# Residual tiles of two projections: loaded plainly ahead of their sums, every product added by VectorE, two kinds of stores issued from other engines

## The chip, the core and the metric

The kernel runs on one core of a Trainium2 chip. The metric is device time in microseconds (us) of one execution, from a median of several runs. The engines are TensorE (PE, with PEld for its weight loads), VectorE (DVE), ScalarE (ACT), GpSimd (POOL) and SyncE (SP). DMAs can be issued from SP, ACT and POOL; each of these issues in the order of its own instruction queue, and an instruction that waits holds up all that stand behind it on the same engine.

## The reference

One layer of a hybrid encoder on 512 tokens of width 2048, all in float32. An mLSTM branch and a differential-attention branch are computed from a common input projection, gated, and mixed; what matters here comes after:

```
x  = x + (g_m * branch_m + g_a * branch_a) @ w_out     # 2048 x 2048, "wo"
h2 = rmsnorm(x, norm2_w)
gate, up = split(h2 @ w_ffn_in)                         # 2048 x 11264, "fi"
x  = x + (silu(gate) * up) @ w_ffn_out                  # 5632 x 2048, "fo"
return rmsnorm(x, final_norm_w)
```

The two lines that begin with `x = x +` are residual sums. Their first operands (the input `x` in the first, the `x` after the first sum in the second) are called residual tiles here: [128 tokens x 512 columns], 16 of them in each sum.

## The kernel before, in words

**Arithmetic.** Every float32 operand is split into a high and a low part of type fp32r: ScalarE casts the high part (line 149), VectorE subtracts it from the source to get the low part (line 150). A product is three matmuls (high x high, high x low, low x high, line 145). Large products are made by `seven`, a seven-product (Strassen-Winograd) scheme over 2x2 blocks: per group of 512 rows of the weight there are the products Q1, Q5, Q6, then Q2, Q3, Q7, and at the end Q4, each 12 matmuls of 128x128x512. Sums of raw weight blocks (lines 348, 356, 362, 369) and of operand blocks are VectorE's.

**Order.** `seven` runs over all groups with Q1, Q5, Q6, then over all groups with Q2, Q3, Q7 (in the last group Q7, Q3, Q2), then over all groups with Q4. Each product accumulates over the groups in one of three pairs of PSUM banks (`BANK`: a for Q1 and Q2, b for Q6, Q7, Q4, c for Q5 and Q3). After the last group of a product, `post` takes the bank's sum away. "wo" has 4 groups, and two chunks (wo0, wo1) of 1024 output columns each. "fo" has 10 groups in the seven-product scheme and an eleventh in plain products (W12, W22, W11, W21, with a further pair of banks d), again in two chunks (fo0, fo1). "fi" lies between wo1 and fo0: 11 chunks.

**Weights.** Raw weight blocks (512 KB each) come by SP's DMAs (line 197) into a ring of buffers, 6 to 8 loads ahead of use; a buffer is free when VectorE has read it last. `take` makes pieces two ahead of use (`AHEAD = 2`).

**Time in the program.** The program's own clock is advanced by each step (`tick`; a product step counts 12 x 216 ns). `later(ns, fn)` puts a step off by so much of that clock, and `when` / `behind` / `work` hand out one small step per product. The instructions on each engine are then put in order by a list scheduler, so neighbours can change places.

**Buffers.** `t_` tiles (128x512, float32) come from one pool of 39; a tile that finds no free one waits for the last reader of an older tile.

**The step that changes.** `added` (line 791) makes `post` for wo and fo. Output blocks are named 11, 12, 21, 22. After Q1, ScalarE copies bank a three times for each of two token tiles (six copies, line 813) into the tiles 22, 12 and 21, with sign; Q5, Q6, Q7, D, Q3, Q4 are added or subtracted by VectorE (lines 816 to 837). The residual tile enters 21 right after Q1, 12 after Q3, and 22 after Q7 (wo) or D (fo), by a DMA from POOL that adds the DRAM tile to the tile in SBUF (`accum_op`, line 802). Block 11 is different: its residual tile is loaded plainly after Q5 (line 817), and Q2 is added to it by VectorE. `final` of the blocks 22 and 12 is put off by `later(8000, ...)`, that of 11 and 21 follows at once.

In wo, `final` stores the sum to DRAM from POOL (`x1d`, line 883), squares it on ScalarE (line 885) and, when two token tiles are there, has `turned` 2 us of program time later: TensorE transposes them (line 849), ScalarE scales them out of PSUM (line 858) and stores them from its own queue (line 860); for the columns of wo0 VectorE makes four sums of the turned blocks (line 863), which SP stores (line 864). wo1 loads these again at its Q2 (line 494, from POOL). In fo, `final` squares on ScalarE (line 1004), multiplies by the final norm's weight, and with the fourth tile of a token row scales and stores the output. During fo POOL also loads fi's results (line 988), each of which is split by ScalarE and VectorE.

Of the kernel before, what the change touches and what calls it, by code (L numbers as in the profile page):

```python
# [14 lines left out]
AF = mybir.ActivationFunctionType  # L15
ALU = mybir.AluOpType
# [11 lines left out]
NFB = DFF // 512  # L28
# [86 lines left out]
def build(ctx, tc, a, out):  # L115
    nc = tc.nc
    V, A, G, T = nc.vector, nc.scalar, nc.gpsimd, nc.tensor
# [97 lines left out]
    def later(ns, fn):  # L215

        tasks.append((clock[0] + ns, fn))
        tasks.sort(key=lambda t: t[0])
# [337 lines left out]
    xs, q, vals, sig, mqk, mval, has, hms = [], {}, {}, {}, {}, {}, [], []  # L556
# [232 lines left out]
    x1d = [[dpool.tile([P, 512], F32, name=f"x1d{t}_{c}") for c in range(4)] for t in range(NT)]  # L789

    def added(nm, n, src, final, plain=False):
        x = {}

        def tile_(q, i):
            x[q, i] = t_(f"{nm}_x{q}{i}")
            return x[q, i]

        def place(q, i):
            return (i if q < 20 else 2 + i), 2 * n + (q - 1) % 10

        def fetch(q, i):
            G.dma_start(x[q, i], src(*place(q, i)), accum_op=ALU.add)

        def end(q, i):
            t, c = place(q, i)
            final(t, c, x[q, i])

        def post(q_, bank):
            a_, b_, c_ = (bank[k] for k in "abc")
            for i in range(2):  # L810
                if q_ == "Q1":
                    for q, sc in ((22, -1.0), (12, -1.0), (21, 1.0)):
                        A.activation(tile_(q, i), a_[i], AF.Copy, scale=sc)
                    fetch(21, i)
                elif q_ == "Q5":
                    V.tensor_tensor(x[22, i], x[22, i], c_[i], ALU.add)  # L816
                    G.dma_start(tile_(11, i), src(*place(11, i)))
                elif q_ == "Q6":
                    V.tensor_tensor(x[12, i], x[12, i], b_[i], ALU.subtract)
                elif q_ == "Q7":  # L820
                    V.tensor_tensor(x[22, i], x[22, i], b_[i], ALU.subtract)
                    if not plain:
                        fetch(22, i)
                        later(8000, lambda i=i: end(22, i))
                elif q_ == "D":
                    V.tensor_tensor(x[22, i], x[22, i], bank["d"][i], ALU.add)
                    fetch(22, i)
                    later(8000, lambda i=i: end(22, i))
                elif q_ == "Q3":
                    V.tensor_tensor(x[12, i], x[12, i], c_[i], ALU.add)  # L830
                    fetch(12, i)
                    later(8000, lambda i=i: end(12, i))
                elif q_ == "Q2":
                    V.tensor_tensor(x[11, i], x[11, i], a_[i], ALU.add)
                    end(11, i)
                else:
                    V.tensor_tensor(x[21, i], x[21, i], b_[i], ALU.add)  # L837
                    end(21, i)
        return post

    def turned(nm, src, cols, out, i, keep, scale=None):

        for j in (1, 2):
            f_ = f"X{i + 1}{j}"
            tp = ps(f"{nm}_T{i}{j}")
            for k in range(2):
                kk = 2 * k + j - 1
                for t in range(2):
                    T.transpose(tp[:, k * 256 + t * P:k * 256 + (t + 1) * P],
                                src[t][:, cols + kk * P:cols + (kk + 1) * P], ident)  # L850
            out[f_] = half(f"{nm}_{f_}")
            tv = tp.rearrange("p (k c) -> p k c", k=2)
            if scale is None:
                A.copy(out[f_], tv)
            else:
                for k in range(2):
                    kk = 2 * k + j - 1
                    A.activation(out[f_][:, k], tv[:, k], AF.Copy, scale=scale(kk))
            if keep and f_ in keep:
                nc.scalar.dma_start(keep[f_].rearrange("p (k c) -> p k c", k=2), out[f_])  # L860
        if keep and "S1" in keep and len(out) == 4:
            def sum_(f_, to, l, r, op):
# [17 lines left out]

    def wo_chunk(n):
        def final(t, c, x):
            G.dma_start(x1d[t][c], x)
            j = t_(f"x1j{t}_{c}")
            A.activation(j, x, AF.Square, accum_out=ss2p[:, t * 4 + c:t * 4 + c + 1])
            x1[t, c] = x
            i = t // 2
            if (2 * i, c) in x1 and (2 * i + 1, c) in x1:
                pair = [x1.pop((2 * i + k, c)) for k in range(2)]
                later(2000, lambda: turned(f"h2{c}", pair, 0, h2X[c], i,  # L890
                                           h2d[c] if n == 0 else None,
                                           lambda kk: n2w[:, c * 4 + kk:c * 4 + kk + 1]))

        def start(q_):
            if n == 1 and q_ == "Q2":
                for g in range(4):
                    h2f[g] = {}
                p0, p1 = (loaded(f"h2{c}", c, h2f[c], h2d[c]) for c in range(2))
                p2, p3 = (kept(f"h2{c}", c, h2f[c], h2X[c]) for c in (2, 3))
                ahead([p0[0], p1[0], p0[1]])  # L900
                for c, p in ((3, p3), (2, p2)):
                    when(lambda c=c: len(h2X[c]) >= 4, p[0])
                when(lambda: True, [p1[1][0]] + p1[1][1])
                when(lambda: True, p3[1] + p2[1])

        seven(f"wo{n}", lambda g, h_, l: a["w_out"][n, g, h_, l], range(4), lambda g: mixf[g],
              added(f"wo{n}", n, lambda t, c: a["x"][t][:, c * 512:(c + 1) * 512], final), start)

    def rstd2():
        ss2 = sm("ss4", NT, bufs=2)  # L910
# [90 lines left out]
    def fo_chunk(n):  # L1001
        def final(t, c, x):
            j = t_(f"x2j{t}_{c}")
            A.activation(j, x, AF.Square, accum_out=ss3p[:, t * 4 + c:t * 4 + c + 1])  # L1004
            mine = fin.setdefault(t, [])
            mine.append((c, x))
            if len(mine) < 4:
                later(0 if n else 30000, lambda: V.tensor_tensor(x, x, env["fnw"][c], ALU.mult))  # L1008
                tick(0)
                return  # L1010
            ss = sm("ss1", 1)
            V.tensor_reduce(ss, ss3p[:, t * 4:t * 4 + 4], AX.X, ALU.add)
# [12 lines left out]
        def start(q_):  # L1025
            if q_ == "Q4" and n == 0:
                env["fnw"] = [t_(f"fnw{c}") for c in range(4)]
                for c in range(4):
                    G.dma_start(env["fnw"][c],
                                a["fnw"][:, c * 512:(c + 1) * 512].broadcast_to([P, 512]))  # L1030
        seven(f"fo{n}", lambda g, h_, l: a["w_ffo"][n, g, h_, l], GR, lambda g: fgf[n, g],
              added(f"fo{n}", n, lambda t, c: x1d[t][c], final, True), start, NFB - 1, True)

    fin = {}

# [281 lines left out]
    for k in range(KD):  # L1317
# [159 lines left out]
```

## Time and profile before

| | |
|---|---|
| time, median of 3 runs | 2661.37 us (2660.05 to 2668.32) |
| the profiled execution, its own time | 2664.15 us |
| its span | 2662.4 us |
| mean granted TensorE clock | 0.994 |
| busy: PE / DVE / ACT / POOL | 2599.0 / 2106.5 / 1308.8 / 253.7 us |
| wo0 and wo1, fi, fo0 and fo1 (from the span's start) | 1158 to 1337, 1337 to 2204, 2204 to 2652 us |

All rows come from the one profiled execution. Times in the timeline are from the span's start. A row of the timeline is: start, duration, engine, line, operation, tile written <- tiles read, shape, and in brackets the engine's idle time before it with what ended that. "x6" says that six neighbours are merged. In a row of the waits stand: who waited <- for whom: us in total, times, longest us. In a row of a window PEclk is the granted share of the TensorE clock, DMA share the mean busy share of the 16 DMA engines.

### The profile page before, as it was taken

How to read it: one execution, taken by the hardware profiler on the slowest of the kernel's cores; microseconds unless marked ns; L12 is line 12 of the kernel's file. 1: busy time of each engine (PE TensorE's matmuls, PEld its weight loads, DVE VectorE, ACT ScalarE, POOL GpSimd, SP SyncE). 2: the span in 40 equal slices, each digit the busy share in tenths (PEclk: the TensorE clock that was granted, in tenths of full speed). 3: DMA queues.
4: the chain of work that ended last, by engine and by line, in shares of the span. 5: the costliest groups of instructions: out<-in, count | busy, mean ns of one | idle time of the engine just before them, and what ended most of it. 6: DMA issues, size and time to landing. Idle time of an engine off the chain costs nothing. (4 is left out here: it accounts for less than half of the span.)

```text
span 2662.4 us, 33245 instructions
## 1 busy us (share of the span) xinstructions
PE 2599.0 (98%) x12184; PEld 2160.8 (81%) x12184; DVE 2106.5 (79%) x2660; ACT 1308.8 (49%) x1848; POOL 253.7 (10%) x448
## 2 busy tenths in 40 slices
PE   7999999999999999998999999999999999999997
PEld 6878888878889988887778888888888878787886
DVE  8977888788875675686788888788888879879885
ACT  8544444545543543354564444444444436646554
POOL 1000000011210122101200000000000001222211
PEclk9999999999999999999999999999999999999999
DMA  7655566744432345447755554565555577777763
GB/s 250 237 187 181 201 200 208 240 119 126 132 104 88 125 158 208 169 150 233 216 203 180 188 195 165 177 211 181 186 190 186 176 281 276 251 256 257 239 224 91
DMA packets 162227, 508.97 MB, mean 191 GB/s; under 512 B 21832, under 2 KB 22120, under 8 KB 162064
## 3 DMA queue, kind: packets, MB, share of 16 engines
q1 hardware_dynamic: 111456, 379.77, 41.6%
q0 software_dynamic: 33712, 97.71, 12.3%
q10 hardware_dynamic: 16896, 29.37, 3.2%
q8 instruction: 95, 1.56, 0.2%
q14 instruction: 68, 0.56, 0.1%
HBM read 445.41 MB, written 50.87 MB: 186 GB/s over the span
## 5 line engine op out<-in xcount | busy, mean ns | idle before, releaser
L145 PE MATMUL aqk_b<-xs,whi_aqk 128*128 128x512 f32 x512 | 161.6, 396 | 0.0
L149 ACT CAST whi_fi_Q<-fi_Q_t 128x1024 fp32r<-128x1024 f32 x88 | 92.5, 1052 | 116.7 <-PE fi_b L145 98.3
L145 PE MATMUL fi_a<-whi_fi_Q,h_X 128*128 128x512 f32 x440 | 147.2, 392 | 0.0
L145 PE MATMUL fi_c<-whi_fi_Q,h_S 128*128 128x512 f32 x440 | 144.6, 390 | 0.0
L145 PE MATMUL fi_b<-whi_fi_Q,h_S 128*128 128x512 f32 x352 | 115.6, 389 | 0.0
L145 PEld LDWEIGHTS aqk_b<-xs,whi_aqk 128*128 128x128 f32 x512 | 94.6, 189 | 18.3
L150 DVE TENSOR_TENSOR wlo_fi_Q<-fi_Q_t,whi_fi_Q 128x1024 fp32r<-128x1024 f32 x88 | 106.2, 1217 | 4.1 <-ACT whi_fi_Q L149 4.1
L362 DVE TENSOR_TENSOR raw_fi_e<-raw_fi_e,raw_fi_f 128x1024 f32<-128x1024 f32 x44 | 53.9, 1224 | 65.0 <-DMA raw_fi_e<-in_w_ffi 64.9
L145 PE MATMUL aqk_b<-xs,wlo_aqk 128*128 128x512 f32 x256 | 100.5, 393 | 0.0
L145 PEld LDWEIGHTS fi_c<-whi_fi_Q,h_S 128*128 128x128 f32 x440 | 82.6, 188 | 17.1
L145 PEld LDWEIGHTS fi_a<-whi_fi_Q,h_X 128*128 128x128 f32 x440 | 82.6, 188 | 16.8
L988 POOL DMA_DIRECT2D fs_X<-fg_X11d x22 | 11.8, 538 | 830.2 <-DVE wlo_fi_Q L150 785.5
L145 PE MATMUL fi_a<-wlo_fi_Q,h_X 128*128 128x512 f32 x220 | 86.0, 391 | 1.9 <-DVE wlo_fi_Q L150 1.8
L348 DVE TENSOR_TENSOR raw_fi_b<-raw_fi_b,raw_fi_a 128x1024 f32<-128x1024 f32 x44 | 53.8, 1223 | 41.5 <-DMA raw_fi_b<-in_w_ffi 36.7
L145 PE MATMUL fi_c<-wlo_fi_Q,h_S 128*128 128x512 f32 x220 | 86.0, 391 | 0.6 <-DVE wlo_fi_Q L150 0.5
L145 PE MATMUL ba_p<-whi_ba,hahl 128*128 128x512 f32 x256 | 82.5, 392 | 0.0
L149 ACT CAST whi_fi_Q<-raw_fi_e 128x1024 fp32r<-128x1024 f32 x44 | 46.4, 1055 | 73.1 <-PE fi_b L145 48.2
L149 ACT CAST whi_fi_Q<-raw_fi_b 128x1024 fp32r<-128x1024 f32 x44 | 46.5, 1056 | 69.5 <-PE fi_c L145 51.9
L145 PE MATMUL bm_p<-whi_bm,hmhl 128*128 128x512 f32 x256 | 80.5, 392 | 0.0
L145 PE MATMUL mqk_b<-xs,whi_mqk 128*128 128x512 f32 x256 | 80.4, 394 | 0.0
L149 ACT CAST whi_fi_Q<-raw_fi_f 128x1024 fp32r<-128x1024 f32 x44 | 46.4, 1055 | 67.4 <-PE fi_c L145 65.3
L145 PEld LDWEIGHTS fi_b<-whi_fi_Q,h_S 128*128 128x128 f32 x352 | 66.1, 188 | 13.6
(837 smaller groups left out, 8452.3 us busy)
## 6 DMA issues: line engine op xcount, KB each, us to landing
raw_fi_a<-in_w_ffi SPq DMA_DIRECT2D x44, 512.0 KB, 3.7
raw_fi_b<-in_w_ffi SPq DMA_DIRECT2D x44, 512.0 KB, 4.2
raw_fi_c<-in_w_ffi SPq DMA_DIRECT2D x44, 512.0 KB, 4.4
raw_fi_d<-in_w_ffi SPq DMA_DIRECT2D x44, 512.0 KB, 4.2
raw_fi_f<-in_w_ffi SPq DMA_DIRECT2D x44, 512.0 KB, 3.8
raw_fi_e<-in_w_ffi SPq DMA_DIRECT2D x44, 512.0 KB, 4.2
raw_aqk<-in_w_aqk SPq DMA_DIRECT2D x32, 512.0 KB, 3.6
raw_fo_a<-in_w_ffo SPq DMA_DIRECT2D x20, 512.0 KB, 4.8
```

The source lines that it names most:

```text
L145: T.matmul(dst, lhs[l], rhs[r], start=first and i == 0, stop=last and i == 2, skip_group_check=skip)
L149: A.copy(hi, src)
L150: V.tensor_tensor(lo, src, hi.bitcast(F32), ALU.subtract)
L348: V.tensor_tensor(raws[r12], raws[r12], raws[r11], ALU.add)
L362: V.tensor_tensor(raws[r12], raws[r12], raws[r22], ALU.add)
L988: G.dma_start(got[n], fgd[g][f_].rearrange("p (k c) -> p k c", k=2))
```

## The change

All six tiles that Q1 goes into are loaded with their residual tiles beforehand, by plain DMAs from POOL, 10 us (wo) or 66 us (fo) of program time after the first Q1 of the chunk; the two tiles of block 11 likewise 12 us or 70 us after the first Q2. VectorE adds or subtracts every product, Q1 too, straight onto them: six VectorE operations in place of six ScalarE copies in each of the four chunks. There is no accumulating DMA and no `later(8000, ...)`: `final` follows the last product of each block at once. `x1d` is stored from ScalarE's queue, behind the square; the four sums of the turned blocks of wo0 are stored from POOL in place of SP.

```diff
     def added(nm, n, src, final, plain=False):
         x = {}
-        def tile_(q, i):
-            x[q, i] = t_(f"{nm}_x{q}{i}")
-            return x[q, i]
...
-        def fetch(q, i):
-            G.dma_start(x[q, i], src(*place(q, i)), accum_op=ALU.add)
+        def fetch(*qs):
+            for q in qs:
+                for i in range(2):
+                    x[q, i] = t_(f"{nm}_x{q}{i}")
+                    G.dma_start(x[q, i], src(*place(q, i)))
+
+        def put(q, i, bank, op):
+            V.tensor_tensor(x[q, i], x[q, i], bank[i], op)
...
                 if q_ == "Q1":
-                    for q, sc in ((22, -1.0), (12, -1.0), (21, 1.0)):
-                        A.activation(tile_(q, i), a_[i], AF.Copy, scale=sc)
-                    fetch(21, i)
+                    put(22, i, a_, ALU.subtract)
+                    put(12, i, a_, ALU.subtract)
+                    put(21, i, a_, ALU.add)
                 elif q_ == "Q5":
-                    V.tensor_tensor(x[22, i], x[22, i], c_[i], ALU.add)
-                    G.dma_start(tile_(11, i), src(*place(11, i)))
+                    put(22, i, c_, ALU.add)
...
                 elif q_ == "Q7":
-                    V.tensor_tensor(x[22, i], x[22, i], b_[i], ALU.subtract)
+                    put(22, i, b_, ALU.subtract)
                     if not plain:
-                        fetch(22, i)
-                        later(8000, lambda i=i: end(22, i))
+                        end(22, i)
                 elif q_ == "D":
-                    V.tensor_tensor(x[22, i], x[22, i], bank["d"][i], ALU.add)
-                    fetch(22, i)
-                    later(8000, lambda i=i: end(22, i))
+                    put(22, i, bank["d"], ALU.add)
+                    end(22, i)
                 elif q_ == "Q3":
-                    V.tensor_tensor(x[12, i], x[12, i], c_[i], ALU.add)
-                    fetch(12, i)
-                    later(8000, lambda i=i: end(12, i))
+                    put(12, i, c_, ALU.add)
+                    end(12, i)
...
-        return post
+        return post, fetch

     def turned(nm, src, cols, out, i, keep, scale=None):
...
-                nc.sync.dma_start(keep[f_].rearrange("p (k c) -> p k c", k=2), to)
+                (G if scale else nc.sync).dma_start(keep[f_].rearrange("p (k c) -> p k c", k=2), to)

     def wo_chunk(n):
         def final(t, c, x):
-            G.dma_start(x1d[t][c], x)
             j = t_(f"x1j{t}_{c}")
             A.activation(j, x, AF.Square, accum_out=ss2p[:, t * 4 + c:t * 4 + c + 1])
+            nc.scalar.dma_start(x1d[t][c], x)
...
         def start(q_):
+            if q_ == "Q1":
+                later(10000, lambda: fetch(22, 12, 21))
+            elif q_ == "Q2":
+                later(12000, lambda: fetch(11))
...
     def fo_chunk(n):
...
         def start(q_):
+            if q_ == "Q1":
+                later(66000, lambda: fetch(22, 12, 21))
+            elif q_ == "Q2":
+                later(70000, lambda: fetch(11))
```

## Rows read from the trace of the kernel before

**Rows 1.** The page, part 1: busy time, share, instructions

```profile
PE 2599.0 (98%) x12184; PEld 2160.8 (81%) x12184; DVE 2106.5 (79%) x2660; ACT 1308.8 (49%) x1848; POOL 253.7 (10%) x448
```

**Rows 2.** Windows: stretch, length, busy PE, PEld, DVE, ACT, POOL, PEclk, DMA share, GB/s

```profile
1250.00:1344.00 94.00, 84.98 (x371) 68.41 (x370) 70.26 (x76) 48.81 (x78) 16.29 (x26) 0.96 0.74 238
2204.00:2421.00 217.00, 210.31 (x918) 170.40 (x917) 188.76 (x213) 125.19 (x172) 47.78 (x85) 1.00 0.77 263
```

**Rows 3.** TensorE's waits, from 1236, 1290, 1338, 2399 and 2625 us

```profile
PE wo_a L145 <- DVE wlo_wo_Q L150: 5.9, 2, 3.3
...
PE wo_a L145 <- ACT whi_wo_Q L149: 1.1, 1, 1.1
...
PE wo_a L145 <- DVE wlo_wo_Q L150: 0.8, 1, 0.8
...
PE h_T L849 <- DVE wo_x L837: 2.5, 2, 2.3
...
PE fo_b L145 <- DVE wlo_fo_Q L150: 2.0, 3, 0.8
PE fo_b L145 <- ACT whi_fo_Q L149: 1.1, 2, 0.6
...
PE fo_b L145 <- ACT whi_fo_Q L149: 3.5, 1, 3.5
```

**Rows 4.** Windows of 10 us with a low PEclk, the first and the last

```profile
1240.00:1250.00 10.00, 6.69 (x27) 5.14 (x26) 7.04 (x8) 7.55 (x17) 1.08 (x2) 0.83 0.77 267
...
2630.00:2640.00 10.00, 9.15 (x32) 7.16 (x33) 5.15 (x5) 4.28 (x5) 0.00 (x0) 0.83 0.24 87
```

**Rows 5.** Timeline of VectorE: sums of weights after their loads

```profile
1242.36 1.23 DVE L348 TENSOR_TENSOR raw_wo_b<-raw_wo_b,raw_wo_a 128x1024 f32<-128x1024 f32 x1 [7.62 <-DMA raw_wo_b<-in_w_out]
...
1337.59 1.22 DVE L348 TENSOR_TENSOR raw_fi_b<-raw_fi_b,raw_fi_a 128x1024 f32<-128x1024 f32 x1 [4.40 <-DMA raw_fi_b<-in_w_ffi]
```

**Rows 6.** The tile raw_wo_b: its eight loads, from issue to landing

```profile
DMA to landing us min/median/max: 3.4/4.4/8.6
```

**Rows 7.** Timeline of ScalarE around 1240 and 1291 us, with a store's issue

```profile
1232.67 0.33 ACTq L860 DMA_DIRECT2D h_X11d<-h_X  x1
...
1240.36 0.63 ACT L885 ACTIVATE x1j<-wo_x 128x512 f32<-128x512 f32 x1 [4.06 <-DMA x1d<-wo_x]
...
1290.92 0.62 ACT L149 CAST h_X<-h_X 128x512 fp32r<-128x512 f32 x1 [5.00 <-DMA h_X<-h_X11d]
```

**Rows 8.** Timeline of POOL after wo1's Q1: first of four adds, first load

```profile
1280.62 0.90 POOL L802 DMA_DIRECT2D wo_x<-in_x  x1 [32.09 <-ACT wo_x L813]
...
1283.57 0.80 POOL L494 DMA_DIRECT2D h_X<-h_X11d  x1
```

**Rows 9.** ScalarE's groups of line 1004 in 2372:2412 and 2616:2632; timeline at 2629

```profile
L1004 ACT ACTIVATE x2j<-fo_x 128x512 f32<-128x512 f32 x6 | 3.7, 624 | 11.2 <-DMA fo_x<-x1d 9.3 <-DVE fo_x L834 1.9
...
L1004 ACT ACTIVATE x2j<-fo_x 128x512 f32<-128x512 f32 x6 | 3.7, 618 | 0.8 <-PE fo_b L145 0.8
...
2629.23 2.94 ACT L149 CAST whi_fo_Q<-fo_Q_t 128x1024 fp32r<-128x1024 f32 x3 [0.41 <-ACT fo_x L1021]
```

**Rows 10.** Timeline: ScalarE's six copies in fo0, a VectorE pair from PSUM

```profile
2283.97 3.05 ACT L813 ACTIVATE fo_x<-fo_a 128x512 f32<-128x512 f32 x6 [0.99 <-PE fo_a L145]
...
2288.04 1.28 DVE L816 TENSOR_TENSOR fo_x<-fo_x,fo_c 128x512 f32<-128x512 f32 x2
```

**Rows 11.** Timeline of VectorE: its next operation after Q1's end, four chunks

```profile
1189.82 1.23 DVE L362 TENSOR_TENSOR raw_wo_e<-raw_wo_e,raw_wo_f 128x1024 f32<-128x1024 f32 x1 [2.50 <-DMA raw_wo_e<-in_w_out]
...
1280.58 1.23 DVE L362 TENSOR_TENSOR raw_wo_e<-raw_wo_e,raw_wo_f 128x1024 f32<-128x1024 f32 x1 [1.56 <-DMA raw_wo_e<-in_w_out]
...
2286.90 1.23 DVE L362 TENSOR_TENSOR raw_fo_e<-raw_fo_e,raw_fo_f 128x1024 f32<-128x1024 f32 x1 [2.66 <-DMA raw_fo_f<-in_w_ffo]
...
2509.57 1.22 DVE L362 TENSOR_TENSOR raw_fo_e<-raw_fo_e,raw_fo_f 128x1024 f32<-128x1024 f32 x1 [2.51 <-DMA raw_fo_f<-in_w_ffo]
```

**Rows 12.** SP's waits from 1150 to 1360 us, one line

```profile
SPq L864 <- DVE h_X L863: 8.6, 6, 4.0
```

More of the change, by code (lines that the diff above doesn't have):

```diff
@@ L792, in added @@
         x = {}
-        def tile_(q, i):
-            x[q, i] = t_(f"{nm}_x{q}{i}")
-            return x[q, i]
         def place(q, i):
             return (i if q < 20 else 2 + i), 2 * n + (q - 1) % 10
-        def fetch(q, i):
-            G.dma_start(x[q, i], src(*place(q, i)), accum_op=ALU.add)
+        def fetch(*qs):
[5 more added lines that the diff above has]
+            V.tensor_tensor(x[q, i], x[q, i], bank[i], op)
         def end(q, i):
-            t, c = place(q, i)
-            final(t, c, x[q, i])
+            final(*place(q, i), x[q, i])
         def post(q_, bank):
@@ L811, in post @@
                 if q_ == "Q1":
-                    for q, sc in ((22, -1.0), (12, -1.0), (21, 1.0)):
-                        A.activation(tile_(q, i), a_[i], AF.Copy, scale=sc)
-                    fetch(21, i)
+                    put(22, i, a_, ALU.subtract)
+                    put(12, i, a_, ALU.subtract)
+                    put(21, i, a_, ALU.add)
                 elif q_ == "Q5":
-                    V.tensor_tensor(x[22, i], x[22, i], c_[i], ALU.add)
-                    G.dma_start(tile_(11, i), src(*place(11, i)))
+                    put(22, i, c_, ALU.add)
                 elif q_ == "Q6":
-                    V.tensor_tensor(x[12, i], x[12, i], b_[i], ALU.subtract)
+                    put(12, i, b_, ALU.subtract)
                 elif q_ == "Q7":
-                    V.tensor_tensor(x[22, i], x[22, i], b_[i], ALU.subtract)
+                    put(22, i, b_, ALU.subtract)
                     if not plain:
-                        fetch(22, i)
-                        later(8000, lambda i=i: end(22, i))
+                        end(22, i)
                 elif q_ == "D":
-                    V.tensor_tensor(x[22, i], x[22, i], bank["d"][i], ALU.add)
-                    fetch(22, i)
-                    later(8000, lambda i=i: end(22, i))
+                    put(22, i, bank["d"], ALU.add)
+                    end(22, i)
                 elif q_ == "Q3":
-                    V.tensor_tensor(x[12, i], x[12, i], c_[i], ALU.add)
-                    fetch(12, i)
-                    later(8000, lambda i=i: end(12, i))
+                    put(12, i, c_, ALU.add)
+                    end(12, i)
                 elif q_ == "Q2":
-                    V.tensor_tensor(x[11, i], x[11, i], a_[i], ALU.add)
+                    put(11, i, a_, ALU.add)
                     end(11, i)
                 else:
-                    V.tensor_tensor(x[21, i], x[21, i], b_[i], ALU.add)
+                    put(21, i, b_, ALU.add)
                     end(21, i)
-        return post
+        return post, fetch
     def turned(nm, src, cols, out, i, keep, scale=None):
@@ L904, in start @@
                 when(lambda: True, p3[1] + p2[1])
+        post, fetch = added(f"wo{n}", n, lambda t, c: a["x"][t][:, c * 512:(c + 1) * 512], final)
         seven(f"wo{n}", lambda g, h_, l: a["w_out"][n, g, h_, l], range(4), lambda g: mixf[g],
-              added(f"wo{n}", n, lambda t, c: a["x"][t][:, c * 512:(c + 1) * 512], final), start)
+              post, start)
     def rstd2():
@@ L1030, in start @@
                                 a["fnw"][:, c * 512:(c + 1) * 512].broadcast_to([P, 512]))
+        post, fetch = added(f"fo{n}", n, lambda t, c: x1d[t][c], final, True)
         seven(f"fo{n}", lambda g, h_, l: a["w_ffo"][n, g, h_, l], GR, lambda g: fgf[n, g],
-              added(f"fo{n}", n, lambda t, c: x1d[t][c], final, True), start, NFB - 1, True)
+              post, start, NFB - 1, True)
     fin = {}
```

## The prediction

> **What bounds the kernel now.** I read the busy shares first, then the stages, then TensorE's waits, then whoever TensorE waited for. The page shows TensorE busy for 2599.0 of 2662.4 us [rows 1]: nothing but its gaps, and the time in which it runs slowly, can be gained. By stage the change touches wo and fo alone. There VectorE is busy for 70.26 of 94 us (75%) in wo1 and for 188.76 of 217 us (87%) in fo0, and ScalarE for 52% and 58% [rows 2]. The change takes work from the emptier of the two and gives it to the fuller, which is the first thing to weigh.
>
> TensorE's gaps in these stages come in five bunches, and I name them for the sum [rows 3]:
> - A and B, in wo1's start: 5.9 us, two waits for low parts of weights.
> - C, at the start of wo1's second phase: four waits, the first 1.1 and the last 0.8, 3.7 us together.
> - D, in fi's start: 2.5 us, transposes that wait for VectorE's last sum.
> - E, near the end of fo0: 2.0 + 1.1 = 3.1 us.
> - F, near the end of fo1: 3.5 us for one cast.
>
> After A, B, C and F the granted clock falls: a 10 us window at 0.83 loses 10 x 0.17 = 1.7 us. There are four such windows (0.83 to 0.86), the first behind A, the last behind F [rows 4]. This time goes only where its gap goes. At stake: A and B 5.9 + 3.4 = 9.3, C 3.7 + 1.7 = 5.4, D 2.5, E 3.1, F 3.5 + 1.7 = 5.2, together 25.5 us.
>
> **The change part by part.**
>
> *The adding DMAs and their delay go.* E is the plainest: ScalarE's squares of fo0 waited 9.3 us for residual tiles to be added by DMA [rows 9], and the casts that TensorE needs stood behind them. In the changed kernel the sum is done when VectorE's last operation is, so this wait is gone: 3.1 of 3.1. What is late next there is the cast's own source, which was ready. At least 2.0 goes, if VectorE's part of E has another cause.
>
> F: six squares (618 ns each) began only after 0.8 us of waiting for a free buffer, and the cast came at 2629.23, behind them and the scaling of the output [rows 9]. Four of the six belong to blocks 22 and 12, which now end with W22, four steps (some 10 us) before Q2's end. 4 x 0.62 + 0.8 = 3.3 of the 3.5 us go, and with so short a gap the slow stretch too: 3.3 + 1.7 = 5.0 (at least 3.3).
>
> A and B: the squares of wo0 waited 4.06 us for an `x1d` store to give back a buffer [rows 7], and VectorE sat 7.62 us until a weight block landed [rows 5]. One of these loads took 8.6 us against a median of 4.4 [rows 6]. It flew together with the adding DMAs of blocks 12 and 22 and with four stores. In the changed kernel the residual loads are over by then, and the stores of 22 and 12 leave 8 us sooner. If the load lands at the median it is 4.2 us earlier, more than the longer wait of 3.3: A goes with its slow window (5.0). B is A's echo, as each weight load is issued when VectorE has let go of a buffer; I take 1.5 of its 4.3. A and B: 6.5 (2.0 to 9.3).
>
> C: ScalarE waited 5.00 us for a reloaded operand [rows 7], which POOL issued at 1283.57, behind four adding DMAs begun at 1280.62 [rows 8]. The load moves up by 2.9 us, and four transfers of 256 KB leave the busiest stretch of wo. More than half of the wait goes; I take 3.5 of 5.4 (1.0 to 5.4).
>
> D: VectorE waited 4.40 us for a weight block [rows 5], and the sum that the transposes need stood behind it. The load flew with the last adding DMAs. 2.0 of 2.5 (0 to 2.5).
>
> Gain taken: 6.5 + 3.5 + 2.0 + 3.1 + 5.0 = 20.1 us, at most 25.5, at least 8.3.
>
> *Q1 goes to VectorE.* Six copies took ScalarE 3.05 us in each chunk. A VectorE pair from PSUM takes 1.28 us, one of them 0.68, so neighbours stand 0.60 apart [rows 10]. Six are 5 x 0.60 + 0.68 = 3.68 us, 14.7 us in four chunks. In front of its next operation VectorE sat idle for 2.50, 1.56, 2.66 and 2.51 us at just these places [rows 11]. What does not fit is 1.18 + 2.12 + 1.02 + 1.17 = 5.5 us, and the low parts for Q2 stand behind it. The scheduler may place them ahead of the sums, and the casts come up to 3.05 us sooner. So 0 to 5.5 us; I take 4.0, nearer to the full row, because VectorE in fo has little room to catch up [rows 2]. A gain here is excluded: the cast was not what VectorE waited for in these rows.
>
> The Trainium skill speaks against this part: "Perfetto Trace Analysis", section "Optimizing Scalar/DVE Operations", says that where VectorE is saturated, work that either engine can do may better go to ScalarE. By that rule this part costs and gives nothing back. The trace agrees half: VectorE is at 87% in fo0, not full [rows 2], and has gaps where the six sums fall [rows 11]. The third rival below gives the rule its chance.
>
> *Stores of x1 from ScalarE.* Sixteen issues at 0.33 us [rows 7] are 5.3 us in its queue; they wait for nothing that the square ahead of them hasn't waited for. Behind each stand casts. ScalarE is half empty [rows 2], and the twelve copies that go from wo were 6.1 us. 0 to 5.3; I take 1.0, for two crowded places where squares, scalings and stores meet.
>
> *Sums of turned blocks from POOL.* SP's queue loses eight stores that waited 8.6 us for VectorE [rows 12] ahead of weight loads; POOL takes these waits, and the residual loads of wo1 stand behind them, more than 10 us ahead of their use. Nothing is taken: the loads behind SP's stores wait for VectorE's buffers anyway. On the transfers themselves nothing is gained either.
>
> The Trainium skill has the same: "DMA: Bandwidth & Descriptors", section "Issuing engines are not separate DMA queues", says that all DMAs share the same 16 engines and that a change of issuer saves only the issuing time. By this rule A, B and D would shrink only by what no longer flies at that moment, which is the second rival's case.
>
> *Loads ahead of Q1.* The same bytes, earlier. Six issues at most 0.90 us each [rows 8] are 5.4 us of POOL's queue. Behind them in fo stand loads of fi's results; TensorE's waits in E and F name weights alone [rows 3], so these loads have room. Nothing, and the fourth rival if the room is missing.
>
> **Sum.** -20.1 + 4.0 + 1.0 = -15.1 us. Against the profiled execution: 2664.15 - 15.1 = 2649.05. That execution lies 2.78 us above the median of the runs, so on the median's scale 2661.37 - 15.1 = 2646.3 us. The own range of this case: 25.5 gained at no cost gives 2635.9; 8.3 gained at costs of 5.5 and 5.3 gives 2663.9, which is not likely all at once, and I end it at 2654.
>
> **Rivals.**
> 1. *Forecast*, 2646.3: chance 0.67.
> 2. *Loads as slow as before.* The weight blocks of A, B, C and D came late because the DMA engines were full (0.74 in wo1 [rows 2]) and because VectorE lets buffers go late, not because of the adds. Then E and F alone go: -3.1 - 5.0 + 5.0 = -3.1, so 2658.3. For it: the same bytes move. Against it: 8.6 against 4.4 us for like loads in one stage [rows 6]. Chance 0.15.
> 3. *VectorE becomes the bound (slower).* The 3.68 us of Q1's sums come ahead of the low parts, every weight load after them is issued so much later because its buffer is let go later, and fo at 87% does not catch up. All 14.7 us fall on TensorE, A to D stay as they are, ScalarE's 5.3 us come on top, and only E and F go: 14.7 + 5.3 - 8.1 = +11.9, so 2673.3. For it: TensorE's waits in A, B and E end mostly on VectorE [rows 3]. Against it: the gaps [rows 11]. It decides once Q1's sums cost TensorE over half of their 3.68 us per chunk and A to D stay. Chance 0.11.
> 4. *The loads are not ahead.* The pool's 39 buffers are short: a square waited 4.06 us for one [rows 7]. If the six tiles find none, POOL stops, Q1's sums wait, bank a isn't free, and TensorE stands at Q2. If at each of four chunks 5 us are lost beside the 15.1 gained: +4.9, so 2666.3. Against it: the program asks some 16 us ahead in wo (ten steps of 2.6 us less 10) and some 6 us ahead in fo (28 steps less 66). Chance 0.07.
>
> **How the numbers follow.** 0.3% of 2661 us is 8 us, about what a measurement of this kernel can tell from no change: bounds 2653.4 and 2669.4. Faster: nearly all of the forecast (0.66) and a little of the second (0.04), 0.70. Same: most of the second and half of the fourth, 0.15. Slower: the third and half of the fourth, 0.15. The range from 2633 to 2661 holds the forecast's own range and the second rival; below 2636 it leaves room for gaps that I have not counted, above it leaves out the third and the fourth.
>
> **What would show it.** Right, step by step: no square on ScalarE waits for a residual DMA; the bunch E is gone; the cast at F comes within 0.5 us of its need, and PEclk stays at full there; weight blocks around A land in under 5 us; the window after C shows no 0.83. Six VectorE sums stand in a row after Q1, and TensorE's wait behind them is under 1.5 us per chunk. Wrong: new waits of TensorE for low parts of 3 us behind Q1, or waits of POOL for buffers ahead of the residual loads. The prediction fails if A to D are still there (second rival), or if TensorE stands longer in fo0 than the 6.7 us that it does now (third) [rows 2].

## The result, and the profile after

The changed kernel takes 2640.36 us (median of 4 runs, 2634.88 to 2640.70); the kernel before took 2660.71 us beside it (4 runs, 2657.53 to 2668.32). The ratio is 0.9915 with a 95% interval of 0.9899 to 0.9930: faster by 22.6 us (18.6 to 26.9) on 2661 us; the medians themselves lie 20.4 us apart. The prediction said 2646.3. The profiled execution took 2640.17 us, with a span of 2637.6 us.

The page's busy times, which answer to [rows 1]:

```profile
PE 2592.7 (98%) x12184; PEld 2160.2 (82%) x12184; DVE 2120.6 (80%) x2684; ACT 1297.7 (49%) x1824; POOL 240.0 (9%) x440
```

VectorE has 14.1 us more work, close to the 14.7 us of Q1's sums that the prediction counted, and ScalarE 11.1 us less. The time came from TensorE's gaps. All its waits of the changed kernel, first from 1150 to 1440 us (wo and fi's start), then from 2180 to 2640 us (fo); columns as in [rows 3]:

```profile
PE wo_b L145 <- DVE wlo_wo_Q L150: 5.7, 2, 4.9
PE wo_a L145 <- DVE wlo_wo_Q L150: 1.7, 2, 0.9
PE wo_b L145 <- ACT whi_wo_Q L149: 1.7, 1, 1.7
PE fg_T L846 <- DVE fu L931: 0.2, 1, 0.2
...
PE fo_b L145 <- DVE wlo_fo_Q L150: 2.4, 4, 1.1
PE fo_b L145 <- ACT whi_fo_Q L149: 0.7, 1, 0.7
```

They sum to 9.3 and 3.1 us. In the kernel before, the same two views sum to 14.0 and 13.6 us; for fo they were:

```profile
PE fo_b L145 <- ACT whi_fo_Q L149: 4.6, 3, 3.5
PE fo_b L145 <- DVE wlo_fo_Q L150: 4.6, 8, 0.8
PE fo_c L145 <- DVE wlo_fo_Q L150: 1.9, 2, 1.0
PE fo_a L145 <- DVE wlo_fo_Q L150: 1.8, 3, 0.8
PE fi_b L145 <- DVE wlo_fi_Q L150: 0.7, 1, 0.7
```

So the waits for a high part (E and F, 4.6 us) shrink to 0.7 us, as predicted, and of the waits for low parts 8.3 us become 2.4. Only 2.0 of these belong to E; the other 6.3 are ten waits of about 1 us and less, most of them in fo's second phases, that no term of the prediction had. From its first product to fi's first, wo takes 173.9 us (before 178.9); from its first product to its last, fo takes 431.6 us (before 445.5). Of the 24.8 us between the two spans, 2.7 lie ahead of wo, where the change does nothing: single executions of the kernels below reach wo between 1152.2 and 1158.5 us.

Two gaps of the changed kernel are left in wo, and both are readable in its timeline (columns as in the rows of the front part):

```profile
1230.71 0.33 SPq L197 DMA_DIRECT2D raw_wo_b<-in_w_out  x1
...
1236.89 1.23 DVE L348 TENSOR_TENSOR raw_wo_b<-raw_wo_b,raw_wo_a 128x1024 f32<-128x1024 f32 x1 [3.63 <-DMA raw_wo_b<-in_w_out]
1238.04 2.35 DVE L150 TENSOR_TENSOR wlo_wo_Q<-wo_Q_t,whi_wo_Q 128x1024 fp32r<-128x1024 f32 x2
...
1259.38 0.54 POOL L494 DMA_DIRECT2D h_X<-h_X11d  x1
...
1268.85 0.62 ACT L149 CAST h_X<-h_X 128x512 fp32r<-128x512 f32 x1 [5.91 <-DMA h_X<-h_X11d]
```

The first is what became of A: a sum of weight blocks waits 3.63 us for its load, and two low parts, whose casts had ended by 1234.7, stand behind it. TensorE waits 4.90 us, longer than at A before (3.3). The second is what became of C: a cast waits 5.91 us for a reloaded operand, and a cast of weights stands behind it. The load starts at 1259.38 us, not at 1283.57 [rows 8], and the wait has moved with it from wo1's second phase to the end of its first. Windows of 10 us behind these two places and at F, and one of fo0's length (columns as in [rows 2]):

```profile
1239.00:1249.00 10.00, 9.69 (x30) 7.74 (x31) 5.66 (x7) 2.65 (x5) 0.00 (x0) 0.69 0.40 137
1270.00:1280.00 10.00, 7.50 (x27) 5.87 (x27) 8.85 (x11) 6.36 (x9) 1.61 (x3) 0.83 0.86 317
2609.00:2619.00 10.00, 8.81 (x38) 6.80 (x38) 5.94 (x5) 4.83 (x5) 0.00 (x0) 1.00 0.29 109
...
2196.00:2413.00 217.00, 215.47 (x948) 176.15 (x947) 199.82 (x227) 125.17 (x169) 46.59 (x87) 1.00 0.78 273
```

The granted clock still falls behind the first two (0.69 and 0.83); at F, where it was 0.83 [rows 4], it is 1.00. In fo0 VectorE is busy for 199.82 of 217 us, 92% after 87%, and TensorE stands for 1.5 us, not for 6.7.

Q1's sums in fo0, with a sum of weight blocks some 9 us ahead of them (VectorE's timeline):

```profile
2267.54 1.22 DVE L362 TENSOR_TENSOR raw_fo_e<-raw_fo_e,raw_fo_f 128x1024 f32<-128x1024 f32 x1 [1.48 <-DMA raw_fo_e<-in_w_ffo]
...
2276.17 3.67 DVE L804 TENSOR_TENSOR fo_x<-fo_x,fo_a 128x512 f32<-128x512 f32 x6
2279.75 1.21 DVE L150 TENSOR_TENSOR wlo_fo_Q<-raw_fo_d,whi_fo_Q 128x1024 fp32r<-128x1024 f32 x1
```

The six sums take 3.67 us in a row, as worked out. In the kernel before, a sum of weight blocks stood at this place and waited 2.66 us for its DMA [rows 11]; now the next such sum comes at 2292.60 and waits for nothing. Behind Q1's sums TensorE waits 0.86 us in wo0 and less than 0.2 us in the other three chunks.

### The profile page after: what moved, and what is told of

The parts are those of the page before. It is cut to its first block, busy times and chain, and to the rows that moved or that the text cites. A ratio compares the mean times of both kernels' runs of the same rounds, so it can differ in the third digit from the quotient of the medians.

```text
span 2637.6 us, 33224 instructions
## 1 busy us (share of the span) xinstructions
PE 2592.7 (98%) x12184; PEld 2160.2 (82%) x12184; DVE 2120.6 (80%) x2684; ACT 1297.7 (49%) x1824; POOL 240.0 (9%) x440
## 3 DMA queue, kind: packets, MB, share of 16 engines
q0 software_dynamic: 31536, 95.62, 11.2%
```

## The experiments

All times in us. "Gain" is 1 minus the ratio, times 2661, with the ratio's interval; each ratio is taken against runs of the kernel before on the same chip.

| kernel | median (range, runs) | ratio to before (95%) | gain |
|---|---|---|---|
| changed | 2640.36 (2634.88 to 2640.70, 4) | 0.9915 (0.9899 to 0.9930) | 22.6 |
| e1, wo only | 2657.10 (2654.33 to 2661.54, 10) | 0.9975 (0.9965 to 0.9985) | 6.7 |
| e9, fo only | 2647.62 (2639.93 to 2656.13, 10) | 0.9952 (0.9936 to 0.9968) | 12.8 |
| e2, Q1 on VectorE only | 2655.09 (2649.80 to 2657.71, 7) | 0.9970 (0.9959 to 0.9982) | 8.0 |
| e3, adds at Q1 only | 2654.07 (2649.70 to 2660.91, 10) | 0.9967 (0.9955 to 0.9980) | 8.8 |
| e5, one sum held | 2656.67 (2650.66 to 2660.50, 10) | 0.9973 (0.9961 to 0.9985) | 7.2 |
| e4, changed, stores as before | 2642.12 (2639.03 to 2644.37, 4) | 0.9923 (0.9907 to 0.9939) | 20.5 |
| e6, changed, Q1's work twice | 2657.55 (2653.15 to 2661.25, 10) | 0.9981 (0.9972 to 0.9991) | 5.1 |
| e7, changed, squares late | 2650.26 (2647.85 to 2652.08, 5) | 0.9955 (0.9940 to 0.9969) | 12.0 |
| e8, changed, three empty steps | 2645.63 (2641.62 to 2650.03, 4) | 0.9939 (0.9920 to 0.9958) | 16.2 |
| e10, changed, one sum held | 2637.92 (2632.30 to 2639.59, 4) | 0.9917 (0.9892 to 0.9943) | 22.1 |
| e11, and casts held | 2635.69 (2631.47 to 2637.79, 4) | 0.9905 (0.9881 to 0.9929) | 25.3 |
| e12, and three sums held | 2637.69 (2636.21 to 2639.51, 5) | 0.9923 (0.9910 to 0.9937) | 20.5 |

**Which stage.** In e1 fo keeps the old `added` (here `added_old`), in e9 wo does, with its stores.

```diff
-        post, fetch = added(f"fo{n}", n, lambda t, c: x1d[t][c], final, True)
+        post = added_old(f"fo{n}", n, lambda t, c: x1d[t][c], final, True)
```

> The change in wo alone (plain loads ahead, Q1's sums on VectorE, stores from ScalarE and GpSimd); fo is as before (six ScalarE copies, adding DMAs, delayed squares). Theory (two parts that add up): the trace of the changed kernel gave about 11 us in wo and fi's start and about 14 us in fo, so this kernel is 9 to 12 us below the kernel before, with E and F (3.1 and 3.5 us of waits near the ends of fo0 and fo1) and the small waits of fo's second phase still there. Rival (the gain of fo comes from wo's, as buffers and loads stand otherwise when fo begins): 18 to 21 us below, and no E or F.

> The change in fo alone; wo with its stores is as in the kernel before. Theory 1 (the stages add up: the whole change gave 20.4 us, wo alone 6.1): 12 to 16 us below the kernel before, with A to D in wo as before and fo as in the changed kernel (about 431 us from its first to its last product). Rival (fo's gain needs wo's part, since buffers or the order of the loads at fo's start depend on it): 7 to 10 us below, E and F gone but small waits in fo's second phases.

wo alone gives 6.7 us (4.0 to 9.3), less than the 9 to 12 expected; fo alone gives 12.8 (8.5 to 17.0), within what its first theory said. Their sum, 19.5, and the whole change's 22.6 lie within the intervals: the stages add up, as far as these runs can tell. In e1's trace E and F are still there (waits for a high part in fo):

```profile
PE fo_b L145 <- ACT whi_fo_Q L149: 5.6, 2, 3.5
```

e9's profiled execution was its slowest run (2656.13 us), with a wait of 3.4 us late in fo1's first phase, where the changed kernel's trace has 0.3; its stage lengths are therefore not used.

**Which part.** e2 moves only the six copies of Q1 to VectorE; e3 keeps them on ScalarE and issues all adding DMAs right behind them, with the squares at once behind the last product.

```diff
 # e2, on the kernel before
-                        A.activation(tile_(q, i), a_[i], AF.Copy, scale=sc)
+                        V.tensor_scalar(tile_(q, i), a_[i], sc, None, ALU.mult)
 # e3, on the kernel before
-                    fetch(21, i)
+                    for q in (22, 12, 21):
+                        fetch(q, i)
```

> One edit of the kernel before: the six copies of Q1 go from ScalarE to VectorE (multiplied by -1 or 1 into the same tiles), with the adding DMAs, delays and stores as they were. Theory 1 (it is VectorE's sums behind Q1 that order its queue anew, weight sums no longer ahead of ready work): fo's small waits, 5.2 us together, go, E and F stay, so 4 to 7 us below the kernel before. Theory 2 (the third rival of the prediction): 3.7 us for each chunk fall on TensorE, some 10 to 15 us above. Theory 3 (Q1's place is of no account): within 2 us.

> The kernel before with ScalarE's copies kept; all three adding DMAs are issued right behind Q1's copies, and the squares of blocks 22 and 12 follow their last product at once. Stores as before. Theory 1 (what counts is that no DMA stands behind the last product): E and F go (8.1 us with F's slow clock) and some of A to C, so 10 to 16 us below the kernel before. Theory 2 (it needs Q1 on VectorE for the rest): 8 to 10 us below, with fo's small waits (5.2 us) still there. Against both: VectorE's sums of Q5 and Q6 would wait for the adding DMAs, if these take longer than a product step of 2.6 us; then gains of under 5 us.

Both parts gain by themselves, 8.0 and 8.8 us. e2 is the surprise: it only adds VectorE work and is faster. Its waits in fo:

```profile
PE fo_b L145 <- ACT whi_fo_Q L149: 5.9, 2, 3.5
PE fo_b L145 <- DVE wlo_fo_Q L150: 3.1, 4, 1.4
PE fo_c L145 <- DVE wlo_fo_Q L150: 0.5, 1, 0.5
```

E and F stay, the waits for low parts fall from 8.3 to 3.6 us: theory 1. Part of this is given back, as E's waits for high parts grow from 1.1 to 2.4 us. In this trace, of e2's fastest run, wo is 3.1 us and fo 2.4 us shorter than before; the other 8.9 us of its shorter span lie ahead of wo and in fi, so the gain is read from the medians alone. In e3 it is the other way round. E and F are gone but for 0.7 us, and the small waits stay (7.8 us for low parts). Three of VectorE's rows in e3, from fo0's Q1 end, show why early adds alone are not the changed kernel:

```profile
2281.77 1.22 DVE L362 TENSOR_TENSOR raw_fo_e<-raw_fo_e,raw_fo_f 128x1024 f32<-128x1024 f32 x1 [2.29 <-DMA raw_fo_f<-in_w_ffo]
2284.51 0.69 DVE L817 TENSOR_TENSOR fo_x<-fo_x,fo_c 128x512 f32<-128x512 f32 x1 [1.52 <-DMA fo_x<-x1d]
...
2289.57 0.69 DVE L817 TENSOR_TENSOR fo_x<-fo_x,fo_c 128x512 f32<-128x512 f32 x1 [1.50 <-DMA fo_x<-x1d]
```

The sum of weight blocks still waits there, and Q5's sums now wait for the adding DMAs, which a load ahead of Q1 avoids.

**Order or relief?** Q1 on VectorE changes two things: ScalarE loses 3.05 us of copies, and VectorE's queue gets another order. e5 keeps the copies on ScalarE and changes only the order: in each chunk of fo one sum of weight blocks, that of Q7's fourth group, must wait for block 12's sum of Q6.

```diff
+        z = sm("held_z", 1)
+        V.tensor_scalar(z, x[12, 0][:, 0:1], 0.0, None, ALU.mult)
+        V.scalar_tensor_tensor(to, to, z, r, ALU.add, ALU.add)
```

> The kernel before with ScalarE's six copies kept. One VectorE operation in each chunk of fo is held back: the sum of two weight blocks (line 362) for the fourth group of Q7, which stood ahead of Q5's sums and waited there up to 2.66 us for its DMA, must now wait for block 12's sum of Q6 (it adds a column of zeros made from that sum). Theory 1 (fo's small waits come of this sum's place in VectorE's queue): they fall from about 6 us to under 3 us, as they did with Q1's sums on VectorE; E and F stay; 2 to 5 us below the kernel before. Rival (they come of ScalarE's 3.05 us of copies, which stand ahead of casts): the small waits stay and the time is within 1 us of the kernel before.

It gains 7.2 us (4.0 to 10.4). VectorE's two rows, and TensorE's waits in fo:

```profile
2294.05 0.15 DVE L795 TENSOR_SCALAR held_z<-fo_x 128x1 f32<-128x1 f32 x1
...
2294.84 1.28 DVE L796 SCALAR_TENSOR_TENSOR raw_fo_e<-raw_fo_e,held_z,raw_fo_f 128x1024 f32<-128x1024 f32 x1
```

```profile
PE fo_b L145 <- ACT whi_fo_Q L149: 5.6, 2, 3.5
PE fo_b L145 <- DVE wlo_fo_Q L150: 2.7, 4, 1.0
...
PE fo_c L145 <- DVE wlo_fo_Q L150: 0.3, 1, 0.3
```

The sum runs 92.7 us behind fo's first product (2202.12), in the kernel before 80.3 us behind it (2206.59), and waits for nothing; the waits for low parts fall from 8.3 to 3.0 us, with ScalarE's copies in place. For these waits it is the order. The time is less certain: the gain is larger than the 2 to 5 us expected, and in this trace fo is only 3.4 us shorter; most of the rest lies ahead of wo and in fi, where VectorE's, ScalarE's and TensorE's instructions stand in the order of before.

How one sum's place reaches that far is in the trace of the kernel before: VectorE's waits for loads from 2278 to 2350 us (fo0's second phase), a place in that phase (ScalarE, then VectorE), and the cast behind Q1's copies.

```profile
DVE raw_fo_e L362 <- DMA raw_fo_e<-in_w_ffo: 5.6, 4, 1.7
DVE raw_fo_e L362 <- DMA raw_fo_f<-in_w_ffo: 2.7, 1, 2.7
...
2321.97 1.06 ACT L149 CAST whi_fo_Q<-raw_fo_f 128x1024 fp32r<-128x1024 f32 x1 [1.15 <-PE fo_c L145]
...
2326.05 1.22 DVE L362 TENSOR_TENSOR raw_fo_e<-raw_fo_e,raw_fo_f 128x1024 f32<-128x1024 f32 x1 [1.54 <-DMA raw_fo_e<-in_w_ffo]
2327.19 1.22 DVE L150 TENSOR_TENSOR wlo_fo_Q<-raw_fo_f,whi_fo_Q 128x1024 fp32r<-128x1024 f32 x1
...
2287.35 1.10 ACT L149 CAST whi_fo_Q<-raw_fo_d 128x1024 fp32r<-128x1024 f32 x1
```

Five sums of weight blocks wait there, 8.3 us together. At 2326.05 a low part whose cast had ended at 2323.03 stands behind such a sum, and TensorE waits 0.86 us for it. In the changed kernel, e2 and e5 no sum of this kind (line 362 before) waits for a load between 2278 and 2350; in e3 four do, 7.0 us together. Right behind Q1 it is otherwise: the low part there has its cast only at 2288.45, after the sum's wait is over (2286.90), so the wait itself holds up no finished cast, and only the sum's own 1.2 us stand in the way. In e5, without the sum at this place, VectorE starts the low part at 2284.16, when its cast has just ended (2283.98), and TensorE's wait of 0.8 us there is gone.

**How much room VectorE has.** e6 adds six more operations of the same size behind Q1's sums in all chunks, into a tile that nobody reads.

```diff
+                    for sc in (-1.0, -1.0, 1.0):
+                        V.tensor_scalar(x["idle"], a_[i], sc, None, ALU.mult)
```

> The changed kernel with VectorE's work behind Q1 doubled: beside the six sums, six more operations of the same size read bank a into a tile that nobody reads, in all four chunks, 14.7 us of VectorE time. Theory 1 (VectorE has room behind Q1, so its sums cost nearly nothing): less than 4 us above the changed kernel. Theory 2 (it has room for six but not for twelve): 4 to 10 us above. Theory 3 (the prediction's term, 1.0 us a chunk, was real but hidden by gains): 4 us above, a wait of 1 us for low parts in each chunk.

None of the theories went far enough. The gain falls from 22.6 to 5.1: 17.5 us in four chunks, 4.4 each, for 3.67 us of work. The first six operations are nearly free, the next six fall on TensorE with a slow clock on top. The 4.4 is a mean: in the traces wo is 3.5 us longer than in the changed kernel, fo 12.4 us. TensorE's waits for low parts in the products of bank a, nearly all of them behind Q1 (1.8 and 3.4 us in wo, 2.8 and 3.0 us in fo), and the windows behind those of wo1 and fo1:

```profile
PE wo_a L145 <- DVE wlo_wo_Q L150: 5.2, 2, 3.4
...
PE fo_a L145 <- DVE wlo_fo_Q L150: 6.5, 3, 3.0
```

```profile
1277.00:1287.00 10.00, 9.30 (x30) 7.47 (x31) 8.40 (x13) 2.27 (x3) 0.00 (x0) 0.69 0.45 156
2508.00:2518.00 10.00, 8.50 (x30) 6.57 (x31) 8.93 (x12) 2.49 (x3) 1.61 (x3) 0.83 0.65 202
```

The granted clock falls to 0.69 and 0.83 there.

**Stores.** e4 takes the changed kernel and puts its stores back: `x1d` from GpSimd ahead of the square, the sums from SP.

> The changed kernel with its stores as before: x1d from GpSimd ahead of the square, the sums of wo0's turned blocks from SP. Theory (the issuing engine is of little account, as the prediction had it, 1.0 us of cost for ScalarE): within 2 us of the changed kernel, so some 20 us below the kernel before. Rival (the sums' stores in SP's queue hold up weight loads, or x1d's stores hold up GpSimd's loads of residual tiles and reloaded operands): 4 to 10 us above the changed kernel, all of it in wo. Other rival (the stores cost the changed kernel its remaining 4.9 us wait in wo1): 4 to 7 us below the changed kernel.

The gains differ by 2.1 us, and the intervals overlap widely: no effect of the stores in sum is measured, as the first theory had it. But within wo the gaps change. The waits at A's place fall to 1.9 us; C's wait for a cast grows from 1.7 to 4.1, because a reloaded operand waits for its store, which SP issues at 1249.37, right behind its sum, and which lands 9.3 us later:

```profile
1264.30 0.62 ACT L149 CAST h_S<-h_S 128x512 fp32r<-128x512 f32 x1 [4.80 <-DMA h_S<-h_S1d]
```

**The delay of the squares.** e7 is the changed kernel with `later(8000, ...)` put back ahead of the ends of blocks 22 and 12.

> The changed kernel with the end of the blocks 22 and 12 (square, store, turning) put off by 8 us of program time, as in the kernel before; no DMA adds. Theory 1 (E was the adding DMA, F the delay): E stays away, F comes back with 2 to 3.5 us and its slow clock, wo is up to 2 us slower; 3 to 6 us above the changed kernel. Theory 2 (the DMA alone made both): within 1.5 us of the changed kernel. Theory 3 (the delay alone made both): 6 to 9 us above, with E's 3 us back.

It costs 10.6 us (22.6 to 12.0). E stays away and F is back to the hundredth, as theory 1 said; TensorE's wait and ScalarE's cast at F in e7:

```profile
PE fo_b L145 <- ACT whi_fo_Q L149: 3.5, 1, 3.5
```

```profile
2613.42 2.94 ACT L149 CAST whi_fo_Q<-fo_Q_t 128x1024 fp32r<-128x1024 f32 x3 [0.41 <-ACT fo_x L1023]
```

Its price was larger than expected, and most of it lies in fo: 8.6 us more than in the changed kernel, where the granted clock stays full from fo's first product to its last. Behind a wait of 2.1 us late in fo1's first phase (0.3 in the changed kernel), and behind F, the windows of e7 are:

```profile
2487.00:2497.00 10.00, 10.00 (x37) 8.11 (x38) 9.05 (x12) 2.85 (x4) 1.07 (x2) 0.83 0.49 158
2613.00:2623.00 10.00, 8.45 (x24) 6.29 (x25) 4.72 (x4) 4.00 (x5) 0.00 (x0) 0.66 0.36 132
```

The wait in fo1's first phase differs from kernel to kernel (3.4 us in e9, 1.4 in e2, less in the others), so it is not put down to the delay. In wo one wait of 6.9 us stands in place of the 4.9, later in wo1's start and again behind a sum that waits for its load; what the delay has to do with it is not shown. So F is the delay. E needs the adding DMAs late: the delay alone does not bring it back, and with the adds right behind Q1 (e3) it is gone.

**Closing the two gaps in wo.** e8 puts three empty steps ahead of the reloaded operands' casts.

```diff
-                ahead([p0[0], p1[0], p0[1]])
+                when(lambda: True, [lambda: None] * 3); ahead([p0[0], p1[0], p0[1]])
```

> The changed kernel with three empty steps ahead of wo1's reloaded operands: their casts come three product steps (7.8 us) later behind the first load. Theory (the wait at 1271.75 in the changed kernel, 2.5 us and its slow clock, is a cast set ahead of its data, 5.9 us early): it goes, 2 to 5 us below the changed kernel. Rival (there is no room: the operands are needed by fi's start, and the wait moves there): within 2 us of the changed kernel or above, with a new wait between 1300 and 1340 us.

It tells nothing on the theory, since the cast did not move: the list scheduler set it at the same place, between the same neighbours, and it waited 5.47 us (5.91 in the changed kernel).

```profile
1265.65 0.62 ACT L149 CAST h_X<-h_X 128x512 fp32r<-128x512 f32 x1 [5.47 <-DMA h_X<-h_X11d]
```

e10 therefore holds an operation by its data, as e5 does: the sum in front of the two low parts (wo1's Q5) waits for the second of these. e11 also holds the first three reloaded operands' casts behind the cast of the last Q6 weights, e12 three more sums.

```diff
 # e10
+        z = sm("held_z", 1)
+        V.tensor_scalar(z, los[after_][:, 0:1].bitcast(F32), 0.0, None, ALU.mult)
+        V.scalar_tensor_tensor(to, to, z, r, ALU.add, ALU.add)
 # e11, besides
+            A.copy(w[0][:, 0, 0:1], his["wo1_Q63"][:, 0:1].bitcast(F32))
 # e12, besides e11: which sum waits for whose low part
-        after_ = {"wo1_Q50": "wo0_Q43"}.get(nm)
+        after_ = {"wo1_Q50": "wo0_Q43", "wo1_Q70": "wo1_Q63", "fo0_Q72": "fo0_Q68", "fo1_Q72": "fo1_Q68"}.get(nm)
```

> The changed kernel with one VectorE operation held back: the sum of the two weight blocks of wo1's Q5, first group, waits (by a column of zeros) for the low part of wo0's last Q4 weights, behind which it belongs in the order of the products. Theory (the wait of 4.90 us at 1239 in the changed kernel is this sum's place ahead of two ready low parts): the wait falls below 1.5 us and its slow clock goes, 3 to 7 us below the changed kernel. Rival (the weight block itself lands too late, so TensorE only waits one product later): a wait of 3 us or more follows within 10 us, and the time is within 2 us of the changed kernel.

> As the kernel with the held sum, and the casts of wo1's first three reloaded operands must stand behind the cast of the last Q6 weights (ScalarE copies one column of these weights into each operand's tile first). Theory (the wait at 1271.75 is a cast set ahead of its data): that wait, 2.5 us and 1.7 of slow clock, goes too, 2 to 4 us below the kernel with the held sum. Rival (the reloaded operands are then late for Q2): a wait of over 1 us for an operand at the start of wo1's second phase, and no gain.

> As the kernel with the held sum and the held casts, and three more sums of weight blocks are held behind low parts that stood behind them: that of wo1's Q7, first group (behind the last Q6 weights), and in each chunk of fo that of Q7, third group (behind Q6, ninth group). Theory (each of TensorE's remaining waits for low parts begins with such a sum that stands ahead of ready work and waits for its DMA): the wait of 4.2 us at 1269 in the kernel with both and the waits of 0.9 us at 2258 and 2475 go, 3 to 7 us below that kernel, some 2630 us. Rival (a held sum only moves the wait to its own product): new waits of the same size within 10 us behind the held sums, and the time within 2 us of the kernel with both.

In e10 the wait of 4.9 us is gone (TensorE's waits from 1150 to 1440 us fall from 9.3 to 6.3), in e11 the wait for a cast too. But each time a further wait appears in wo1. In e11 and e12 it is one of 4.2 and 4.3 us behind a sum that stands ahead of ready low parts. In e12 (SP's and VectorE's timeline) it is:

```profile
1262.98 0.33 SPq L207 DMA_DIRECT2D raw_wo_d<-in_w_out  x1
...
1273.48 1.23 DVE L379 TENSOR_TENSOR wo_Q_t<-wo_Q_t,raw_wo_d 128x1024 f32<-128x1024 f32 x1 [6.32 <-DMA raw_wo_d<-in_w_out]
```

The sum that was held in e12 (line 189 there) is not the one that waits; the next one is. Its load takes 10.5 us from issue to landing, the longest of that tile's eight loads, and the DMA engines are full in that time (e12's loads of the tile, and a window):

```profile
DMA to landing us min/median/max: 3.4/3.6/10.5
...
1263.00:1273.50 10.50, 8.59 (x38) 6.76 (x37) 3.47 (x4) 6.91 (x12) 3.28 (x7) 1.00 1.02 398
```

The waits that the theories of e10 and e11 named went. Of the three of e12's theory, the two of 0.9 us in fo went and the one of 4.2 us in wo1 did not: there the rival holds. The times (gains 22.1, 25.3 and 20.5, with intervals 7 to 14 us wide) are not told apart from the changed kernel's 22.6. In the traces wo is shorter, 167.7, 167.8 and 169.2 us, against 173.0 to 176.1 in the changed kernel, e1, e4 and e8, which leave the sum of wo1's Q5 in its place; these are single executions, e10's and e11's the fastest of their runs, so a gain is suggested, not measured. e11 has the lowest median, 2635.69 us; that it beats the changed kernel is not shown.

## Why the prediction was right, and where it was wrong

The forecast came out 5 us short of the gain in the medians (15.1 against 20.4). The mechanism was right for E and F. It was wrong for A and for Q1's sums and half right for C, and that the number still came so near is partly luck: wo gave less than was forecast and fo more. Of the prediction's own signs, E's end, the full clock at F and the six sums in a row came; a weight block under 5 us around A and a window without 0.83 after C did not.

- **E and F** (predicted -8.1): right. E's squares wait for no DMA now: in the window around E the six squares' idle is 3.6 us and all of it VectorE's, against 11.2 us, 9.3 of it for DMA [rows 9].

```profile
L1006 ACT ACTIVATE x2j<-fo_x 128x512 f32<-128x512 f32 x6 | 3.7, 625 | 3.6 <-DVE fo_x L804 3.6
```

  At F four of the six squares are done by 2598.6, 10 us ahead of the cast (2608.78); TensorE waits 0.66 us for it in place of 3.5, and the clock stays up. That F is the delay's is shown by e7; that E needs the late adding DMA, by e7 and e3 together.
- **A and B** (predicted -6.5): the mechanism named for A was a late load, and that is only a part of it. The load still takes 6.2 us at worst, 8.6 before [rows 6], and TensorE's wait is longer than before. What makes TensorE wait is that VectorE's queue has the sum that needs this load ahead of low parts whose casts are done; e10 moved the sum and the wait went. B, the echo, is gone. Of 9.3 us with the slow windows, 4.9 + 3.1 = 8.0 are left, so 1.3 of the 6.5 came.
- **C** (predicted -3.5): half right. The load did move up, by 24 us and not by 2.9, but the cast moved up with it, and 2.5 us of waits and a slow window (1.7) are left, so 1.2 of the 3.5 came. **D** (predicted -2.0): gone, all 2.5 us, as in e1, e3, e4 and e7, while e2, e5 and e9, with the late adds in wo, have 1.6 to 2.9 us there; whether by the load, as predicted, no run separates.
- **The stages in sum**: in wo, -12.0 for A to D, and half of Q1's cost and the stores against it, makes -9.0 predicted; e1 measured -6.7 (4.0 to 9.3). In fo, -8.1 for E and F and the other half of Q1's cost makes -6.1; e9 measured -12.8 (8.5 to 17.0).
- **VectorE's Q1 sums** (predicted +4.0, between 0 and 5.5): this is the step that failed. "A gain here is excluded" was wrong. The idle of [rows 11] was indeed room: the six sums fit with 0.9 us of wait at most, where the prediction had 5.5 us that do not fit. But the argument stopped at that place. With the six sums there, the sum of weight blocks goes later and finds its data, and so do those that follow it in fo0's second phase; in the kernel before these five waited 8.3 us, a finished cast behind one of them at 2326.05. The term measured -8.0 (4.8 to 10.9, e2), and e5 takes away the same waits by the order, without any of Q1's work being moved. That fo's small waits came of this I had not seen, because I had gathered only the five large bunches.
- **Stores** (predicted +1.0): within what can be measured (e4, 2.1 us between gains). The Trainium skill's "DMA: Bandwidth & Descriptors", section "Issuing engines are not separate DMA queues", says that a change of issuer saves only issuing; in sum e4 agrees, while the gaps inside wo changed size.
- **Loads ahead** (predicted 0): no wait of Q1's sums for a residual tile is in the trace, and the fourth rival fell.
- **The third rival**, VectorE as the bound, was nearer than its chance of 0.11 says. In the changed kernel's fo0 VectorE is at 92%, and six operations behind Q1 cost next to nothing; e6 shows that the next six cost more than their own length in the mean (4.4 against 3.67 us a chunk). The Trainium skill's "Perfetto Trace Analysis", section "Optimizing Scalar/DVE Operations", says that where VectorE is saturated, moving some work to ScalarE may make sense. The first six do not bear this out, the next six agree with it.

## What to carry to other kernels

An engine's idle time ahead of an operation that waits for a DMA can be more than room: look at what stands behind that operation in the queue, whether its inputs are ready, and who waits for it. Where an operation that depends on a load stands ahead of work that is ready, it can be held back by a tiny data dependency; in fo that alone took away as many of the waits for low parts (e5, 8.3 to 3.0 us) as moving Q1's sums to another engine (e2, 8.3 to 3.6). Gather the many waits of 1 us and less too; in fo they held 6.3 us here, more than E or F.

## What the runs showed that was not expected

- More work on a nearly full engine made the kernel faster: e2 adds some 14 us to VectorE and gains 8.0 us.
- 3.67 us of VectorE work behind Q1 cost next to nothing, 7.3 us cost 4.4 us per chunk in the mean, more in fo than in wo. Where between the two the cost begins was not run.
- A load of 512 KB in wo1's middle took 10.5 us from issue to landing in e12, where the median of that tile's loads is 3.6 us, in a stretch in which the DMA engines' busy share is 1.02. With one gap closed in wo, the next load is the next gap (e10 to e12); how much of that is the loads' traffic and how much their late issue stays open.
- Empty steps in the program did not move an operation in the queue (e8), a dependency did (e5, e10, e11).
